# A hand-written timetable taken through the change of token halves, operand blocks replaced in pairs, and the gelu moved behind a copy

## The chip, the core and the metric

The kernel runs on one core of one Trainium2 chip. The metric is device time in microseconds of one execution, the median of three runs; 2668.45 us before the change.

## What is computed

One layer of a hybrid encoder on 2048 tokens of width 1024, in float32. After a mixer (three head groups and an output projection) comes a gated convolutional MLP, and it is there that the change lies:

```python
def conv_ffn(x, w_up, conv_w, conv_b, w_down):
    u = causal_dwconv(x @ w_up, conv_w, conv_b)      # width 3 along the tokens
    g, v = jnp.split(u, 2, axis=-1)                  # 2816 columns each
    return (jax.nn.gelu(g) * v) @ w_down
```

## The kernel before, in words

The up-projection `x @ w_up` is `phase_u` (from L1551). Its work is cut into 44 **units**: two halves of 1024 tokens, 22 column blocks in each (`NFF` = 22), in the order 0, 11, 1, 12, ..., 10, 21. A unit multiplies one block of weights with one half of the tokens, by Winograd's variant of Strassen's scheme: seven products instead of eight, on operands named a11, a12, a22 (blocks of the tokens) and s1, s2, s4, s3 (their sums, stored earlier in DRAM as `summed`), with weights b11, b21, T4, T1, T2, b22, T3 (T1 to T4 are differences). Each operand is held as a high part (`hi`, made by ScalarE, ACT) and a low part (`lo`, the rest, made by VectorE, DVE, or GpSimd, POOL), and each product of 4 x 128 rows is three matmuls per row block (`split3`, L108 to L110), so a unit is 7 x 4 x 3 = 84 matmuls. Results go to PSUM banks X, Y, V and Z. X is used three times and Z twice in a unit: ACT copies a bank out (`keep`, L1775: p1, p5, u2, u3) before the next product may overwrite it. DVE adds the rest (`evac`, L1785). Then come the convolution (ACT L1801, four DVE taps L1741 or L1743), gelu (ACT L1814), the gate product (DVE L1817), and, on every second unit, four sums for the down-projection (L1854 to L1866) and the stores to `aS` (L1632).

The order of all this is written by hand: `steady(first, end)` collects events with a time in ticks (28 ticks are one unit), sorts them by that time, and issues them in that order under `manual_schedule`. The ticks are no clock: they fix only the order of the instructions in each engine's queue, and every engine takes its queue strictly in that order. For unit n, with t0 = 28n and t1 = 28(n + 1), `unit_events` puts the copy p5 at t0 + 16, the copy u2 at t0 + 20, the first bank sum that needs u2 at t0 + 24.2; and, in the next unit's time, gelu at t1 + 13, the gate at t1 + 15.2 and the store of the gated block at t1 + 17. `weight_events` loads and splits the weights of the next unit in the same way; `aux_events` makes, beside chosen units, the operand sums of the second half (units `PRE_U`) and the differences of w_down (22 blocks, one in each of units 20 to 41, `PRE_D_AT`).

This timetable covers units 1 to 20 and 23 to 42. Unit 0 and the last are special. The two around the change of halves, 21 and 22, are `single` units: their seven products run in another order (s1, s2, s4, s3 first; `Product.unit` with `sums_first`), and their instructions are ordered by the general scheduler. While unit 21 runs, `next_half(n)` is called after each product and replaces the operand just used by that of the second half: 28 blocks of 128x512, each loaded, split into hi and lo. The operands have one buffer each, so a block can be replaced only once unit 21 has read it, and must be ready when unit 22 needs it.

Loads go through SyncE's (SP's) queue, and land in shared buffers: four of 512 KB (tag `raw`), six of 256 KB (tag `T`).

Of the kernel before, what the change touches and what calls it, by code (L numbers as in the profile page):

```python
# [18 lines left out]
TH = 1024  # L19
# [3 lines left out]
NFF = DFF // P  # L23
# [39 lines left out]
def tile_hymba_layer(ctx: ExitStack, tc: tile.TileContext, io, out, scr):  # L63
    nc = tc.nc
# [397 lines left out]
    late = []  # L462
# [942 lines left out]
    first = phase_i()  # L1405
# [145 lines left out]
    def phase_u(prod, post_14, post_15):  # L1551
# [12 lines left out]
        def next_half(n):  # L1564

            if n[0] == "s":
                prod.summed_of(1, n)
            else:
                for k in range(4):
                    prod.block(1, k, n, nc.gpsimd if k % 2 else nc.vector)  # L1570

        wT = dram.tile([NFF, P, 4, 512], F32, name="wT", tag="wT")
        w = prod.weights(uw, io["wup_u"][0], "uw0_0", False, ("b21", "b22"), save=wT[0])
        prod.summed_of(0, "s1")
# [131 lines left out]
                for u in range(2):  # L1706
                    products(0, u, (j,))

        def prediffs(ps_, j):

            r, t = (
                rp.tile([P, 4, 256], F32, name=f"p{ps_}_{j}{n}", tag="raw", bufs=prod.raws) for n in "rT"
            )
            nc.sync.dma_start(r, io["wdn"][ps_, j])
            winograd_diffs(t, r[:, 0], r[:, 3], r[:, 1], r[:, 2])
            return lambda: nc.sync.dma_start(scr["diffs"][ps_, j], t)

        order = [b for j in range(NJ) for b in (j, NJ + j)]
        N = NHALF * NFF
        W_ = {0: w}  # L1720
# [2 lines left out]
            half, at = divmod(n, NFF)  # L1723
            return half, at, order[at], f"u{half}_{order[at]}"

        def sums_first(n):
            return n in (NFF - 1, NFF)

        def prepare(n):

            half, _, b, _ = where(n)
            first = sums_first(n)
            W_[n] = prod.weights(
                uw, io["wup_u"][b], f"uw{half}_{b}", first, ("T4",) if first else (),
                wT[b] if half else None, None if half else wT[b],
            )

        def conv_taps(half, u, c, blk, sh):
# [11 lines left out]
        def unit_events(n, at):  # L1750
# [73 lines left out]
            at(t1 + 6.3, tap, 1, 2)  # L1824
            at(t1 + 8.3, tap, 0, 1)
            at(t1 + 10.2, tap, 0, 2)
            at(t1 + 13, gelu)
            at(t1 + 15.2, gate)
            for t, f in operand_steps(half, b, st):
                at(t1 + t, f)  # L1830

        def operand_steps(half, b, st):

            j = b % NJ
            h = slice(0, 4)
# [36 lines left out]

            if b < NJ:
                return [(17, keep)]
            return [(17, store_blocks), (17.2, s3), (18.2, s1), (19.2, s2), (22, s4), (25, store_sums)]

        def weight_events(n, at):

            half, pos, b, _ = where(n)
            nm = f"uw{half}_{b}"  # L1880
            t0 = 28 * (n - 1)
            w = W_[n] = {}
            st = {}

            def load():
                for name, ks in (("ra", slice(0, 2)), ("rb", slice(2, 4))):
                    st[name] = rp.tile([P, 2, 512], F32, name=nm + name, tag="raw", bufs=prod.raws)
                    nc.sync.dma_start(st[name], io["wup_u"][b, :, ks])
                st.update(b11=st["ra"][:, 0], b21=st["ra"][:, 1], b22=st["rb"][:, 0], b12=st["rb"][:, 1])

            def load_t():
                for i in (3, 0, 1, 2):
                    t = rp.tile([P, 512], F32, name=f"{nm}T{i + 1}", tag="T", bufs=prod.raws + 2)
                    nc.sync.dma_start(t, wT[b, :, i])
                    st[f"T{i + 1}"] = t
# [18 lines left out]
            early = 5 if sums_first(n) else 0  # L1914
            if half:
                at(t0 - 28 + 21, load_t)
            else:
                at(t0 + 1.7 - early, diff, "T1", "b12", "b11")
                at(t0 + 2.4 - early, diff, "T2", "b22", "T1")
                at(t0 + 3.1 - early, diff, "T4", "T2", "b21")  # L1920
                at(t0 + 12.2 - 2 * early, diff, "T3", "b22", "b12")
                at(t0 + 5.1, store_t, 1, 2, 4)
                at(t0 + 13.1, store_t, 3)
            names = ("T1", "T2", "b22", "T3", "b11", "T4", "b21") if early else (
                "b11", "b21", "T4", "T1", "T2", "b22", "T3"
            )
            for i, (name, th, tl) in enumerate(zip(
                names, (-1, 2.5, 5, 7, 11, 15, 19), (0, 4.0, 6.2, 8.2, 12.1, 16.5, 20.2)
            )):
                at(t0 + th, hi, name)  # L1930
                at(t0 + tl, lo, name, nc.vector if i else nc.gpsimd)

        def aux(n):


            half, at = divmod(n, NFF)
            if half == 0 and at in PRE_U:
                return "sums", PRE_U.index(at)
            if 0 <= n - PRE_D_AT < len(PRE_D):
                return "diffs", PRE_D[n - PRE_D_AT]  # L1940
            return None

        def aux_events(n, at):
# [48 lines left out]
            at(t0 + 26, make)  # L1992
            at(t0 + 28 + 3, store)

        def steady(first, end):

            ev = []
# [7 lines left out]
                    aux_events(n, at)  # L2005
            for n in range(first + 1, end + 1):
                weight_events(n, at)
            with tc.manual_schedule():
                for _, _, f, args in sorted(ev, key=lambda e: e[:2]):
                    f(*args)  # L2010

        def single(n, after):

            half, at, b, nm = where(n)
            store = None
            if aux(n):
                store = prediffs(*aux(n)[1]) if aux(n)[0] == "diffs" else None
            if n + 1 not in W_:
                prepare(n + 1)
            res = []  # L2020
            for c_, blk in zip(prod.unit(prod.hp, W_[n], nm, after, sums_first(n)), (b, NFF + b)):
# [9 lines left out]
            sums_ = operand(half, b, ug)  # L2031
            for st in (store, sums_):
                if st is not None:
                    st()
# [343 lines left out]
```

## Time and profile before

| what | value |
|---|---|
| median of three runs (lowest, highest) | 2668.45 us (2665.23, 2673.2) |
| the profiled execution's own time | 2669.64 us |
| its span, first to last instruction | 2667.9 us |
| mean granted TensorE clock (1 = full) | 0.974 |
| busy: PE, DVE, ACT, POOL | 93%, 76%, 52%, 30% of the span |
| units 2 to 20, 21 to 23, 24 to 43 of the up-projection | 379.54, 87.97, 403.13 us |

An engine's busy time is the union of its instructions; "idle before" is the time an engine stood still ahead of an instruction, with what released it. Where two neighbouring instructions of one engine overlap in the trace, the start-to-start distance is what the queue pays. A name such as `u_9p` is the tile p of column block 9: digits behind the name are left out, so p1 and p5 both read `u_9p`, and u2 and u3 `u_9u`.

### The profile page before, as it was taken

The numbers are of one execution on the slowest core, as the hardware profiler recorded it, in microseconds if no ns is written. First come the engines' busy times: TensorE is split into PE (matmuls) and PEld (weight loads), VectorE is DVE, ScalarE is ACT, GpSimd is POOL, SyncE is SP. The second block draws the span as 40 slices with busy tenths as digits, with TensorE's granted clock in tenths as the row PEclk, the third lists the DMA queues.
The fourth block names the chain that finished last, engine by engine and source line by source line (L and its number), as shares of the span: only waits on it lengthen the run. The fifth ranks groups of instructions, "written<-read, shape, count | busy, mean of one in ns | idle before, by whom it ended". The sixth has DMA issues, their size and how long they took to land.

```text
span 2667.9 us, 38630 instructions
## 1 busy us (share of the span) xinstructions
PE 2469.9 (93%) x13658; PEld 2122.9 (80%) x13658; DVE 2015.5 (76%) x3086; ACT 1396.6 (52%) x2472; POOL 792.4 (30%) x636
## 2 busy tenths in 40 slices
PE   8899989899888899999899999889999998999997
PEld 8677877778788878878687777677777778999997
DVE  6898689857889864465888888878787877557676
ACT  5556555544567775555544544544444445445343
POOL 5554444434344431132300000521111143003222
PEclk9899989999999999999999999899999999999999
DMA  7444643246666564575545555665666558768776
GB/s 248 147 153 138 206 153 114 93 143 197 169 170 188 169 202 156 172 254 186 192 140 193 183 164 186 225 213 193 207 198 206 194 189 309 236 205 270 272 261 204
DMA packets 316115, 513.55 MB, mean 192 GB/s; under 512 B 23649, under 2 KB 199009, under 8 KB 315921
## 3 DMA queue, kind: packets, MB, share of 16 engines
q1 hardware_dynamic: 314928, 507.94, 58.9%
q8 instruction: 107, 1.75, 0.3%
q0 software_dynamic: 704, 2.10, 0.2%
q10 hardware_dynamic: 288, 1.05, 0.1%
q14 instruction: 88, 0.71, 0.1%
HBM read 343.49 MB, written 167.51 MB: 192 GB/s over the span
## 4 chain that ended last, share of the span: by engine, by line
PE 24%; DVE 13%; DMA 8%; issue 5%; ACT 4%; POOL 1%; SPq 0%; DVEq 0%; ACTq 0%; POOLq 0%
DMA e_10a<-aS 1%; PE e_4b L110 1%; PE mix L109 1%; PE mix L110 1%; PE mix L108 1%; PE e_4b L108 1%; PE e_7b L108 1%; PE e_4b L109 1%; PE e_7b L109 1%; PE e_7b L110 1%; DVE e_6l L2100 1%; PE e_3b L110 1%; PE e_3b L108 0%; PE e_3b L109 0%; PE e_2b L110 0%
## 5 line engine op out<-in xcount | busy, mean ns | idle before, releaser
L996 POOL TENSOR_TENSOR yn<-yn,yg 128x512 f32<-128x512 f32 x16 | 21.6, 1352 | 145.1 <-DMA yg<-gate 103.5
L2190 POOL TENSOR_TENSOR o<-o,y 128x512 f32<-128x512 f32 x14 | 24.6, 1758 | 126.6 <-DVE y L2189 25.4
L108 PE MATMUL mix<-wo,ym 128*128 128x512 f32 x128 | 51.8, 405 | 1.6 <-DVE ysl L1027 1.6
L110 PE MATMUL mix<-wo,ym 128*128 128x512 f32 x128 | 51.0, 398 | 0.0
L109 PE MATMUL mix<-wo,ym 128*128 128x512 f32 x128 | 50.6, 395 | 0.0
L109 PE MATMUL mix<-wol,ysh 128*128 128x512 f32 x128 | 50.4, 394 | 0.1
L110 PE MATMUL mix<-woh,ysl 128*128 128x512 f32 x128 | 50.0, 390 | 0.0
L108 PE MATMUL mix<-woh,ysh 128*128 128x512 f32 x128 | 49.7, 393 | 0.1
L2084 POOL TENSOR_TENSOR d_0l<-d_0r,d_0h 128x768 fp32r<-128x768 f32 x2 | 4.2, 2104 | 145.6 <-DVE e_6y L2166 144.2
L1509 DVE TENSOR_TENSOR bh<-hT,g 128x512 f32<-128x512 f32 x32 | 20.7, 686 | 34.0 <-PE hT L1508 34.0
L1027 DVE TENSOR_TENSOR ym<-yT,ym 128x512 fp32r<-128x512 f32 x16 | 11.0, 689 | 35.6 <-ACT ym L1026 35.6
L2100 DVE TENSOR_TENSOR e_10l<-e_10a,e_10h 128x896 fp32r<-128x896 f32 x15 | 16.4, 1091 | 25.5 <-ACT e_10h L2099 25.5
L998 DVE TENSOR_TENSOR yn<-yn,yg 128x1024 f32<-128x1024 f32 x16 | 21.3, 1332 | 18.5 <-ACT yg L997 18.5
L2099 ACT ACTIVATE e_8h<-e_8a 128x896 fp32r<-128x896 f32 x15 | 14.3, 954 | 38.6 <-DMA e_8a<-aS 30.1
L851 ACT ACTIVATE no<-n 128x256 f32<-128x256 f32 x64 | 23.9, 375 | 16.2 <-PE n L110 7.0
L1498 ACT ACTIVATE bt<-bx 128x1024 f32<-128x1024 f32 x16 | 16.9, 1058 | 29.4 <-DVE bx L1497 29.4
L627 PE MATMUL xT<-ident,x 128*128 128x128 f32 x128 | 20.4, 306 | 12.5 <-DVE x L621 8.4
L628 DVE TENSOR_TENSOR hT<-xT,par 128x512 f32<-128x512 f32 x32 | 21.4, 683 | 13.6 <-PE xT L627 13.6
L2100 DVE TENSOR_TENSOR e_6l<-e_6a,e_6h 128x896 fp32r<-128x896 f32 x15 | 23.8, 1589 | 8.3 <-ACT e_6h L2099 8.3
L1270 DVE SCALAR_TENSOR_TENSOR s_1L<-s_1A,gt,nmask 128x128 f32<-128x128 f32 x64 | 29.2, 482 | 1.0 <-PE s_1pp L1330 0.9
L2100 DVE TENSOR_TENSOR e_9l<-e_9a,e_9h 128x896 fp32r<-128x896 f32 x15 | 16.4, 1091 | 17.5 <-ACT e_9h L2099 17.5
L2100 DVE TENSOR_TENSOR e_5l<-e_5a,e_5h 128x896 fp32r<-128x896 f32 x15 | 23.9, 1596 | 7.4 <-ACT e_5h L2099 7.3
(9832 smaller groups left out, 10909.4 us busy)
## 6 DMA issues: line engine op xcount, KB each, us to landing
x<-in_x_dram SPq DMA_DIRECT2D x16, 512.0 KB, 4.9
hT<-hT SPq DMA_DIRECT2D x16, 512.0 KB, 4.2
gate<-no SPq DMA_DIRECT2D x64, 128.0 KB, 3.0
yn<-yns SPq DMA_DIRECT2D x16, 512.0 KB, 4.6
yg<-gate SPq DMA_DIRECT2D x16, 512.0 KB, 4.9
bx<-in_x_dram SPq DMA_DIRECT2D x16, 512.0 KB, 4.3
x<-bx SPq DMA_DIRECT2D x16, 512.0 KB, 2.9
h2T<-bh SPq DMA_DIRECT2D x16, 512.0 KB, 4.9
```

The costliest lines, as they stand in the source:

```text
L108: a = nc.tensor.matmul(pss, lh, rh, start=first, stop=False, skip_group_check=True)
L109: nc.tensor.matmul(pss, lh, rl, start=False, stop=False, skip_group_check=True)
L110: nc.tensor.matmul(pss, ll, rh, start=False, stop=last, skip_group_check=True)
L627: nc.tensor.transpose(pt[:, j * P : (j + 1) * P], xt[:, k * P : (k + 1) * P], ident)
L628: nc.vector.tensor_tensor(hT[:, 4 * q : 4 * q + 4], pt.rearrange("p (a b) -> p a b", a=4), col(par, "g1", 4 * q, 4).unsqueeze(2).to_broadc ...
L851: nc.scalar.activation(o, pt[:, 0:256], AF.Copy)
L996: nc.gpsimd.tensor_tensor(yn[:, 512:], yn[:, 512:], g[:, 512:], op=ALU.mult)
L998: nc.vector.tensor_tensor(yn, yn, g, op=ALU.mult)
L1270: nc.vector.scalar_tensor_tensor(L[j][:, hd, :], A[:, hd, j, :], ga[:, hd, 2 * g0 + j : 2 * g0 + j + 1], nmask, op0=ALU.subtract, op1=ALU.add,
L1509: nc.vector.tensor_tensor(hT[:, q * 4 : q * 4 + 4, :], pt.rearrange("p (a b) -> p a b", a=4), g2[:, 4 * q : 4 * q + 4].unsqueeze(2).to_bro ...
L2100: nc.vector.tensor_tensor(al, a, ah.bitcast(F32), op=ALU.subtract)
L2190: nc.gpsimd.tensor_tensor(o[i][:, hs], o[i][:, hs], t, op=ALU.add)
```

## The change

Five things:

1. `steady(1, N - 1)` now covers units 1 to 42 without a break. The two `single` units around the change of halves and their other order of products go.
2. A new `next_half(at)` puts the replacement of the 28 operand blocks into the timetable, as 14 pairs, 3.5 ticks apart, from tick 2.2 of unit 21. A pair's load is issued 7 ticks before its first hi; of every three pairs two use a `raw` buffer, one two `T` buffers; 23 lo parts go to DVE and 5 to POOL.
3. Gelu moves from t1 + 13 to t1 + 16.4, behind p5 and ahead of u2; the gate from 15.2 to 18; the store of the gated block from 17 to 19.5; the sums close up between 19.6 and 22.
4. In the second half the loads of the weight differences are issued one by one (T4, T1, T2, T3 at t0 - 5, - 3, + 1, + 8) instead of together, and the second weight load leaves out b12, which is not used there. For units 22 to 24 the weight loads come later.
5. The differences of w_down are made beside units 16, 18, 19 and 23 to 41 instead of 20 to 41.

The diff, cut to its core:

```diff
-PRE_D, PRE_D_AT = [(i, j) for i in range(2) for j in range(11)], 20
+PRE_D = [(i, j) for i in range(2) for j in range(11)]
+PRE_D_AT = (16, 18, 19) + tuple(range(23, 42))
...
-            at(t1 + 13, gelu)
-            at(t1 + 15.2, gate)
+            at(t1 + 16.4, gelu)
+            at(t1 + 18, gate)
...
-            return [(17, store_blocks), (17.2, s3), (18.2, s1), (19.2, s2), (22, s4), (25, store_sums)]
+            return [(19.5, store_blocks), (19.6, s3), (20.2, s1), (20.8, s2), (22, s4), (25, store_sums)]
...
-            at(t0 - 28 + (9 if aux(n - 3) else 2), load)
+            late = NFF <= n <= NFF + 2
+            t_load = t0 - 28 + (9 if aux(n - 3) else 2)
+            at(t0 - 9 if late else t_load, load, "ra", slice(0, 2), ("b11", "b21"))
+            at(
+                t0 - 2 if late else t_load + 0.1, load, "rb", slice(2, 3 if half else 4),
+                ("b22",) if half else ("b22", "b12"),
+            )
             if half:
-                at(t0 - 28 + 21, load_t)
+                for i, t in ((4, -5), (1, -3), (2, 1), (3, 8)):
+                    at(t0 + t, load_t, i)
...
+        def next_half(at):
+            for i in range(14):
+                name, ks = ("a11", "a12", "a22", "s1", "s2", "s4", "s3")[i // 2], (2 * (i % 2), 2 * (i % 2) + 1)
+                t = 28 * (NFF - 1) + 2.2 + 3.5 * i
...
+                at(t - 7, load)
+                at(t, hi, 0)
+                at(t + 0.9, hi, 1)
+                at(t + 0.9, lo, 0, nc.vector)
+                at(t + 1.8, lo, 1, nc.gpsimd if i % 3 == 1 else nc.vector)
...
         single(0, finish_b)
-        steady(1, NFF - 1)
-        single(NFF - 1, next_half)
-        single(NFF, None)
-        steady(NFF + 1, N - 1)
+        steady(1, N - 1)
```

## Rows read from the trace of the kernel before

**Rows 1.** Page: span of the profiled execution

```profile
span 2667.9 us, 38630 instructions
```

**Rows 2.** Windows: stretch, length, PE, PEld, DVE, ACT, POOL busy, PEclk, DMA, GB/s

```profile
1307.93:1687.47 379.54, 370.77 (x1598) 301.33 (x1597) 325.57 (x418) 178.34 (x303) 26.61 (x19) 0.99 0.52 170
1687.47:1775.44 87.97, 70.53 (x254) 52.64 (x252) 71.06 (x74) 42.47 (x71) 50.69 (x33) 0.83 0.75 247
1775.44:2178.57 403.13, 391.71 (x1683) 314.20 (x1682) 324.09 (x393) 188.67 (x324) 57.32 (x47) 1.00 0.61 198
```

**Rows 3.** Windows of single units of the up-projection

```profile
1404.46:1423.77 19.31, 19.31 (x86) 15.78 (x85) 14.76 (x19) 9.43 (x16) 1.29 (x1) 1.00 0.62 203
1443.07:1468.37 25.30, 22.30 (x85) 17.66 (x84) 17.43 (x23) 9.31 (x16) 1.27 (x1) 0.87 0.71 233
1566.52:1589.01 22.49, 19.61 (x86) 15.69 (x85) 17.44 (x23) 9.31 (x16) 1.29 (x1) 1.00 0.80 258
1627.62:1648.85 21.23, 19.64 (x85) 15.70 (x84) 20.38 (x27) 9.32 (x16) 1.68 (x1) 1.00 0.60 199
1706.75:1752.12 45.37, 28.69 (x85) 19.07 (x83) 42.94 (x44) 22.66 (x36) 26.91 (x16) 0.74 0.74 246
1752.12:1775.44 23.32, 22.56 (x85) 17.79 (x85) 12.19 (x14) 9.51 (x19) 14.08 (x10) 0.84 0.65 220
1814.14:1834.30 20.16, 19.62 (x86) 15.69 (x84) 17.58 (x24) 9.32 (x16) 2.42 (x3) 1.00 0.56 181
1834.30:1854.30 20.00, 19.61 (x86) 15.69 (x84) 15.04 (x19) 9.32 (x16) 2.39 (x3) 1.00 0.72 236
```

**Rows 4.** Waits of PE outside the switch: total, times, longest

```profile
PE u_15Z L108 <- ACT u_15p L1775: 3.0, 1, 3.0
...
PE u_17Z L108 <- ACT u_17p L1775: 1.5, 1, 1.5
```

**Rows 5.** Waits of PE, 1690 to 1775 us

```profile
PE u_11X L108 <- ACT uw_11b11h L131: 6.6, 1, 6.6
PE u_0W L109 <- DVE uS_3s4l L133: 5.4, 1, 5.4
```

**Rows 6.** Timeline of unit 18: start us, length, engine, line

```profile
1639.76 1.27 DVE L1743 SCALAR_TENSOR_TENSOR u_19v<-u_19ca,upar,u_19v 128x1022 f32<-128x1022 f32 x1
1641.12 1.06 ACT L1814 ACTIVATE u_19v<-u_19v 128x1024 f32<-128x1024 f32 x1 [4.76 <-DVE u_19v L1743]
1642.09 0.61 ACT L1908 ACTIVATE uw_20b22h<-uw_20rb 128x512 fp32r<-128x512 f32 x1
1642.61 0.58 ACT L1775 ACTIVATE u_9p<-u_9Z 128x512 f32<-128x512 f32 x1
1643.24 0.50 PE L108 MATMUL u_9Z<-uS_0s4h,uw_9b22h 128*128 128x512 f32 x1 [1.59 <-ACT u_9p L1775]
1643.61 0.59 ACT L1775 ACTIVATE u_9u<-u_9X 128x512 f32<-128x512 f32 x1
```

**Rows 7.** Timeline of DVE in unit 30

```profile
1894.22 0.42 DVE L99 TENSOR_TENSOR x29t<-x29r 128x256 f32<-128x256 f32 x1 [1.02 <-DMA x29r<-in_wdn_dram]
1895.71 1.40 DVE L102 TENSOR_TENSOR x29t<-x29t,x29r 128x256 f32<-128x256 f32 x1
...
1908.28 1.23 DVE L1817 TENSOR_TENSOR u_14v<-u_14v,u_14v 128x1024 f32<-128x1024 f32 x1 [0.52 <-ACT u_14v L1814]
...
1912.88 0.69 DVE L1866 TENSOR_TENSOR u_14v<-u_14v,u_3v 128x512 f32<-128x512 f32 x1
```

**Rows 8.** Line L133, 1690 to 1776 us: min/median/max ns

```profile
L133 POOL TENSOR_TENSOR uw_0T2l<-uw_0T,uw_0T2h x1: 1472/1472/1472, 1697.9 to 1697.9; 128x512 fp32r<-128x512 f32 x1
...
L133 DVE TENSOR_TENSOR uA_0a11l<-uA_0a,uA_0a11h x1: 679/679/679, 1711.3 to 1711.3; 128x512 fp32r<-128x512 f32 x1
...
L133 DVE TENSOR_TENSOR uA_2a11l<-uA_2a,uA_2a11h x1: 1768/1768/1768, 1716.2 to 1716.2; 128x512 fp32r<-128x512 f32 x1
```

**Rows 9.** DMA issues, 1776 to 2179 us: KB, us to landing

```profile
aS<-us SPq DMA_DIRECT2D x10, 256.0 KB, 6.9
```

More of the change, by code (lines that the diff above doesn't have):

```diff
@@ L1563, in phase_u @@
         prod.sp, prod.rp, prod.kp = us.get, rp, up
[L1564 to L1570, printed above, removed]
         wT = dram.tile([NFF, P, 4, 512], F32, name="wT", tag="wT")
@@ L1724, in where @@
             return half, at, order[at], f"u{half}_{order[at]}"
-        def sums_first(n):
-            return n in (NFF - 1, NFF)
         def prepare(n):
             half, _, b, _ = where(n)
-            first = sums_first(n)
             W_[n] = prod.weights(
-                uw, io["wup_u"][b], f"uw{half}_{b}", first, ("T4",) if first else (),
-                wT[b] if half else None, None if half else wT[b],
+                uw, io["wup_u"][b], f"uw{half}_{b}", diffs=wT[b] if half else None, save=None if half else wT[b]
             )
@@ L1873, in operand_steps @@
             if b < NJ:
-                return [(17, keep)]
-            return [(17, store_blocks), (17.2, s3), (18.2, s1), (19.2, s2), (22, s4), (25, store_sums)]
+                return [(19.5, keep)]
+            return [(19.5, store_blocks), (19.6, s3), (20.2, s1), (20.8, s2), (22, s4), (25, store_sums)]
         def weight_events(n, at):
@@ L1883, in weight_events, with load, load_t @@
             st = {}
[L1885 to L1895, printed above, removed]
+            def load(name, ks, names):
+                t = rp.tile([P, 2, 512], F32, name=nm + name, tag="raw", bufs=prod.raws)
+                nc.sync.dma_start(t[:, 0 : ks.stop - ks.start], io["wup_u"][b, :, ks])
+                st.update((n, t[:, i]) for i, n in enumerate(names))
+            def load_t(i):
+                t = rp.tile([P, 512], F32, name=f"{nm}T{i}", tag="T", bufs=prod.raws + 2)
+                nc.sync.dma_start(t, wT[b, :, i - 1])
+                st[f"T{i}"] = t
             def diff(name, x, y):
@@ L1911, in lo @@
                 eng.tensor_tensor(w[name][1], st[name], w[name][0].bitcast(F32), op=ALU.subtract)
-            at(t0 - 28 + (9 if aux(n - 3) else 2), load)
-            early = 5 if sums_first(n) else 0
+            late = NFF <= n <= NFF + 2
[5 more added lines that the diff above has]
+            )
             if half:
-                at(t0 - 28 + 21, load_t)
-            else:
[L1918 to L1921, printed above, removed]
+                for i, t in ((4, -5), (1, -3), (2, 1), (3, 8)):
+                    at(t0 + t, load_t, i)
+            else:
+                at(t0 + 1.7, diff, "T1", "b12", "b11")
+                at(t0 + 2.4, diff, "T2", "b22", "T1")
+                at(t0 + 3.1, diff, "T4", "T2", "b21")
+                at(t0 + 12.2, diff, "T3", "b22", "b12")
                 at(t0 + 5.1, store_t, 1, 2, 4)
                 at(t0 + 13.1, store_t, 3)
-            names = ("T1", "T2", "b22", "T3", "b11", "T4", "b21") if early else (
-                "b11", "b21", "T4", "T1", "T2", "b22", "T3"
-            )
             for i, (name, th, tl) in enumerate(zip(
-                names, (-1, 2.5, 5, 7, 11, 15, 19), (0, 4.0, 6.2, 8.2, 12.1, 16.5, 20.2)
+                ("b11", "b21", "T4", "T1", "T2", "b22", "T3"),
+                (-1, 2.5, 5, 7, 11, 15, 19), (0, 4.0, 6.2, 8.2, 12.1, 16.5, 20.2)
             )):
@@ L1938, in aux @@
                 return "sums", PRE_U.index(at)
-            if 0 <= n - PRE_D_AT < len(PRE_D):
-                return "diffs", PRE_D[n - PRE_D_AT]
+            if n in PRE_D_AT:
+                return "diffs", PRE_D[PRE_D_AT.index(n)]
             return None
@@ L1993, in aux_events, with load, hi, lo @@
             at(t0 + 28 + 3, store)
+        def next_half(at):
+            for i in range(14):
+                name, ks = ("a11", "a12", "a22", "s1", "s2", "s4", "s3")[i // 2], (2 * (i % 2), 2 * (i % 2) + 1)
+                nm = f"uB{name}{ks[0]}"
+                st = {}
+                t = 28 * (NFF - 1) + 2.2 + 3.5 * i
+                def load(name=name, ks=ks, nm=nm, st=st, split=i % 3 == 2):
+                    if split:
+                        st["r"] = [
+                            rp.tile([P, 512], F32, name=f"{nm}r{q}", tag="T", bufs=prod.raws + 2) for q in range(2)
+                        ]
+                    else:
+                        r = rp.tile([P, 2, 512], F32, name=nm + "r", tag="raw", bufs=prod.raws)
+                        st["r"] = [r[:, q] for q in range(2)]
+                    if name[0] == "s":
+                        src = prod.summed[1, int(name[1]) - 1, :, ks[0] : ks[1] + 1]
+                    else:
+                        y, x = int(name[1]) - 1, int(name[2]) - 1
+                        src = prod.src[
+                            4 * x + ks[0] : 4 * x + ks[1] + 1, :, TH + 512 * y : TH + 512 * y + 512
+                        ].rearrange("k p t -> p k t")
+                    if split:
+                        for q in range(2):
+                            nc.sync.dma_start(st["r"][q], src[:, q])
+                    else:
+                        nc.sync.dma_start(r, src)
+                def hi(q, name=name, ks=ks, nm=nm, st=st):
+                    pool = prod.sp(name) if name[0] == "s" else prod.hp
+                    prod.H[ks[q]][name] = [
+                        pool.tile([P, 512], F32R, name=f"{nm}{q}{x}", tag="H" + name, bufs=8) for x in "hl"
+                    ]
+                    nc.scalar.activation(prod.H[ks[q]][name][0], st["r"][q], AF.Copy)
+                def lo(q, eng, name=name, ks=ks, st=st):
+                    h, l = prod.H[ks[q]][name]
+                    eng.tensor_tensor(l, st["r"][q], h.bitcast(F32), op=ALU.subtract)
+                at(t - 7, load)
[3 more added lines that the diff above has]
+                at(t + 1.8, lo, 1, nc.gpsimd if i % 3 == 1 else nc.vector)
         def steady(first, end):
@@ L2007, in steady @@
                 weight_events(n, at)
+            next_half(at)
             with tc.manual_schedule():
@@ L2014, in single @@
             half, at, b, nm = where(n)
[L2015 to L2019, printed above, removed]
+            prepare(n + 1)
             res = []
-            for c_, blk in zip(prod.unit(prod.hp, W_[n], nm, after, sums_first(n)), (b, NFF + b)):
+            for c_, blk in zip(prod.unit(prod.hp, W_[n], nm, after), (b, NFF + b)):
                 res.append(
@@ L2030, in single @@
             nc.vector.tensor_tensor(ug, ug, uv, op=ALU.mult)
[L2031 to L2034, printed above, removed]
+            operand(half, b, ug)
         single(0, finish_b)
-        steady(1, NFF - 1)
-        single(NFF - 1, next_half)
-        single(NFF, None)
-        steady(NFF + 1, N - 1)
+        steady(1, N - 1)
         last(W_[N - 1], where(N - 1)[3], 1, where(N - 1)[2])
```

7 lines of the change are left out of this document (removed).

## The prediction

> **What bounds the kernel now.** I read the page for the span [rows 1], then the busy time by stretch [rows 2], then single units [rows 3], then what PE waited for [rows 4, 5], and last the timelines behind the two kinds of wait [rows 6, 7].
>
> In the up-projection PE sets the pace. An undisturbed unit takes 19.31 us with PE busy all of it [rows 3], so a tick is worth 19.31 / 28 = 0.69 us. What a stretch takes beyond that is loss [rows 2]: units 2 to 20 lose 379.54 - 19 x 19.31 = 12.7 us; units 21 to 23, around the change of halves, 87.97 - 3 x 19.31 = 30.0 us; units 24 to 43 lose 403.13 - 20 x 19.31 = 16.9 us. Together 59.6 us, and only there can the change gain.
>
> The 12.7 and 16.9 us have one cause: PE waits at bank Z for p5, up to 3.0 us in the first half and 1.5 us in the second [rows 4]. Unit 18 shows why [rows 6]. It starts at 1627.62. Z is complete at tick 16, at 1638.7, and PE needs it empty at tick 20, at 1641.4. But ACT has gelu ahead of p5; gelu stands behind the last tap on DVE and starts at 1641.12, 13.5 us into the unit. Then come gelu, one hi and p5, which ends at 1643.19, and PE has stood for 1.59 us.
>
> The 30.0 us are another thing [rows 5]: PE waits for the new operands' low parts (5.4 us for one of them) and 6.6 us for the weights of unit 23. In unit 22 PE is busy 28.69 of 45.37 us at a granted clock of 0.74, and in unit 23 the clock is 0.84 [rows 3].
>
> **Gelu behind p5.** No work is added; ACT's queue is reordered. p5 can now run at tick 16, 2.8 us before it is due: this wait goes. Next in line is u2. It waits for tick 20 and is due at tick 24, 16.55 us into the unit, and ahead of it now stand gelu (0.97 us start to start), a hi (0.52 us) and its own 0.59 us [rows 6]. So gelu may start as late as 16.55 - 2.08 = 14.5 us. Unit 18's 13.5 us passes. Unit 9 waited 1.4 us more than unit 18 (3.0 against 1.6), so its gelu came at about 14.9 and u2 would be 0.4 us late; unit 15, with 22.49 - 19.61 = 2.9 us idle [rows 3], likewise. In the second half no wait is above 1.5 us, so every gelu there passes. The gate moves back with gelu; two low parts of DVE now run before it instead of waiting behind it, so DVE loses nothing.
>
> The store of the gated block now leaves two sums closer to s4, which overwrites its source. Now s4 begins 3.4 us after the gate's end without a wait [rows 7]; one instruction of 0.69 us fewer lies between, so DVE may stand 0.7 us on every second unit. DVE is busy 17.58 us in such a unit of 20.16 [rows 3], so that is hidden.
>
> **Differences beside units 16, 18, 19.** Each costs DVE 1895.71 + 1.40 - 1894.22 = 2.9 us [rows 7]. Unit 18's stretch already has DVE busy 20.38 of 21.23 us. Bounds: nothing (units 16 and 20 absorb it) to 2.9 us once; I take 1, nearer to nothing because units whose predecessor keeps only a block have 19.31 - 14.76 = 4.6 us of DVE free [rows 3].
>
> **Loads of the differences T and of b22.** T4, T1, T2 keep 10 ticks, 6.9 us, between load and hi, T3 11 ticks; a 256 KB transfer to DRAM lands in 6.9 us there [rows 9]. I cost them at 0 to 3 us over the half and take 2; the cover is that spacing, and without it T1's low part and all taps behind it on DVE slip. b12 left out saves 256 KB a unit and no time.
>
> So the first half gains 12.7 - 0.8 - 1 = 10.9 us and the second 16.9 - 2 = 14.9 us.
>
> **The change of halves.** The seven products run in their usual order, and a pair is due 2 ticks after the one before it but made 3.5 ticks after it: pair 0 has some 25 ticks in hand, pair 13 about 5, or 3.7 us. The question is DVE. One unit's regular work on it, with the 2.8 us of w_down differences (which units 20 to 22 no longer make) taken out, is 15.04 - 2.8 = 12.2 us, or 17.58 - 2.8 = 14.8 us with the four sums [rows 3, 7]; units 21 and 22 together 27.0 us. The 28 blocks add 23 low parts at 0.68 us [rows 8] = 15.6 us. The five on POOL are not free: a low part on DVE beside one on POOL took 1.77 us, not 0.68 [rows 8], so each may hold DVE up 1.1 us, 5.5 us in all. The sum is 27.0 + 15.6 + 5.5 = 48.1 us of work for 2 x 19.31 = 38.6 us. Nearly all of it stands ahead of pair 13's low parts, so PE stops about 9.5 us in all, in the later products of unit 22 (first through gelu and u2, whose taps are late, then through the operands). ACT is no bound: 2 x 9.32 us [rows 3] and 28 hi parts of 0.52 us make 33.2 of 38.6 us. Stops cost clock: unit 9 stood 3.0 us and lost 6.0 at a clock of 0.87, unit 15 stood 2.9 and lost 3.2 at 1.00 [rows 3]; I add 3 us. SP's loads stand behind the gated block's store and wait for buffers that DVE frees, 0.5 us more. The 6.6 us for weights go: these now have a whole unit of lead. Residue 13 us of 30.0, a gain of 17.
>
> Bounds of the residue: below, 27.0 + 28 x 0.61 (start to start of such parts without POOL in the way) - 38.6 = 5 us, less 3 if the waits that DVE now has between conv and taps are filled: 2 us. Above, every second low part blocked as in [rows 8]: 27.0 + 28 x 1.2 - 38.6 = 22 us, and 5 for the clock: 27 us.
>
> The Trainium skill, "SBUF — State Buffer", section "Who interferes with whom", speaks against the five parts on POOL: a DVE operation with two SBUF inputs and a GpSimd one exclude each other for the whole instruction, the later waits. By that, five POOL instructions of 1.47 us [rows 8] would hold DVE for 7.4 us, not 5.5, and the time would be 2 us higher.
>
> **Sum.** 10.9 + 14.9 + 17.0 = 42.8 us off. The profiled execution took 2669.64 us (span 2667.9 [rows 1] and 1.7 us around it), 1.2 us above the median shown. 2669.64 - 42.8 - 1.2 gives 2625.6; I say 2626 us. With the residues' bounds, (12.7 - 4) + (16.9 - 5) + 3 = 24 to 12.7 + 16.9 + 28 = 57.6 us off, it would be 2611 to 2645.
>
> **Rivals.**
> - *The replacement hides wholly.* DVE fills its present gaps (it idles 87.97 - 71.06 = 17 us in the three units even now [rows 2]) and POOL holds nothing up. Against: 27.0 + 15.6 alone is 4 us over. Gain 10.9 + 14.9 + 28: 2615 us.
> - *The switch gains almost nothing.* A pair's buffer is freed only by its low part, the next load waits for the buffer, and a late DVE delays loads, hi parts on ACT and so its own next work. For it: 44 instructions kept DVE busy 42.94 us in unit 22 [rows 3]. Against: that included sums on another order. It decides once a pair takes over 12 ticks from load to low part. Gain 25.8 + 3: 2640 us.
> - *Gelu moves the stall instead of removing it.* If the taps slip by over 1 us in most units, u2 takes p5's place and the two halves gain nothing: 17 us off, 2651 us. For it: DVE's new neighbours. Against: 13.5 us where 14.5 is allowed.
> - *Slower: s4 stands behind the store.* Place: DVE's s4, every second unit, now closer behind the gated block's store. In unit 30 that store had landed within 3.4 us of the gate's end [rows 7], but other stores to the same tensor took 6.9 us [rows 9]. At 6.9, s4 waits 4 us, gelu comes some 3 us later and u2 is up to 2 us late: 20 such units lose 40 us, just what the halves and switch gain. It turns the sign when the store needs over about 8 us: 43 us are to be eaten, 2.2 us in each. At 9 us: 60 us lost, 2685 us.
> - *The change does not do what it says* (the queues keep their old order): none of the times moves, 2668 us. The sort by ticks speaks against it.
>
> **How the numbers follow.** Forecast 0.52; hidden wholly 0.18; switch gains nothing 0.14; stall moved 0.06; slower 0.06; no effect 0.04. A measurement of this kernel can tell about 0.3%, 8 us, from no change. All cases but the last two are faster by more: 0.90; same 0.04; slower 0.06. The range 2609 to 2645 holds the first three cases with their bounds, some 0.82.
>
> **What would show it.** Right: no wait of PE for p5 or u2 above 0.5 us; units 2 to 20 and 24 to 43 within 2 us of 39 x 19.31; unit 21 at 19 to 20.5 us, unit 22 at 29 to 33 us with PE waiting for low parts of s2, s4 and s3, or for u2; unit 23 near 19.3. Wrong: PE waits for u2 in most units; DVE idle on a DMA before s4; unit 22 under 23 us, or over 40.

## The result, and the profile after

The changed kernel takes 2642.22 us (median of four runs, 2638.97 to 2645.18) against 2670.1 us of the kernel before beside it (2665.23 to 2673.2): a ratio of 0.9881, 95% interval 0.9859 to 0.9904, so about 28 us faster. The forecast was 2626 us, the range 2609 to 2645: the sign and the range held, the size was 16 us too good.

All of it lies in the up-projection. The windows of the three stretches, and below them of single units, after the change (columns as in [rows 2]):

```profile
1312.47:1687.89 375.42, 369.60 (x1598) 300.55 (x1597) 325.77 (x424) 180.69 (x303) 28.03 (x21) 1.00 0.56 179
1687.89:1764.18 76.29, 65.55 (x254) 50.95 (x252) 60.31 (x77) 43.84 (x79) 20.49 (x10) 0.91 0.71 233
1764.18:2150.51 386.33, 386.33 (x1683) 315.64 (x1682) 309.90 (x394) 193.45 (x324) 52.96 (x47) 1.00 0.62 195
...
1447.62:1468.99 21.37, 19.60 (x86) 15.70 (x85) 18.48 (x25) 9.42 (x16) 1.74 (x1) 1.00 0.70 228
1565.52:1589.06 23.54, 21.20 (x86) 16.87 (x85) 18.48 (x25) 9.42 (x16) 1.68 (x1) 0.93 0.74 229
1687.89:1713.75 25.86, 22.22 (x85) 17.60 (x84) 21.59 (x29) 16.89 (x30) 8.77 (x3) 0.87 0.88 284
1713.75:1744.49 30.74, 23.64 (x85) 17.29 (x84) 25.16 (x31) 17.30 (x33) 9.69 (x6) 0.90 0.62 210
1744.49:1764.18 19.69, 19.69 (x86) 16.06 (x84) 13.56 (x18) 9.65 (x16) 2.03 (x2) 0.98 0.63 202
```

Less 19.31 us a unit (19.307 unrounded, which moves a stretch's loss by 0.1 us at most), the stretches now lose 8.5 us (units 2 to 20), 18.4 (21 to 23) and 0.2 (24 to 43, where PE is busy in every microsecond); before it was 12.7, 30.0 and 16.9 [rows 2]. That is 32.6 us off. Units 21 to 23, with the change of halves in them, are called the switch from here on. The span shrank by 30.8 us: the part ahead of unit 2, in which no instruction changed, came out 4.5 us longer in this execution, the rest 2.7 us shorter. The start of unit 2 lay between 1307.9 and 1326.1 us in the executions of this study, so below the kernels are compared by these three losses, and the total stands beside them. The changed kernel and two of the experiments (e4, e7) have the same instructions in units 2 to 20; they lost 8.5, 7.6 and 8.1 us there, so a difference under 1 us between two single executions says nothing.

What is left shows in PE's waits after the change, first outside the switch, then in it (total, times, longest; compare [rows 4, 5]):

```profile
PE u_18X L109 <- ACT u_18u L1754: 2.3, 1, 2.3
PE u_15X L109 <- ACT u_15u L1754: 1.8, 1, 1.8
PE u_20X L109 <- ACT u_20u L1754: 1.6, 1, 1.6
...
PE u_21Z L109 <- ACT u_21p L1754: 3.6, 1, 3.6
PE u_0X L110 <- DVE uBs320l L2015: 3.6, 1, 3.6
PE u_0Z L110 <- DVE uBs400l L2015: 2.0, 1, 2.0
```

No wait for p5 (bank Z) is left outside the switch. In its place stand three for u2 (bank X), in units 9, 15 and 19. In the switch, unit 21 waits for p5, and unit 22 for low parts of s4 and s3.

The timeline around unit 9 shows where u2's lateness begins. Queue of SP, then DVE, ACT and PE, after the change (start us, length, engine, line):

```profile
1441.32 0.37 SPq L1955 DMA_DIRECT2D x8r<-h2T  x1
1441.79 0.40 SPq L1955 DMA_DIRECT2D x8t<-h2T  x1
1442.64 0.37 SPq L1625 DMA_DIRECT2D aS<-u_14v  x1
...
1449.16 0.69 DVE L1845 TENSOR_TENSOR u_14v<-u_14v,u_3v 128x512 f32<-128x512 f32 x1 [2.93 <-DMA aS<-u_14v]
...
1463.82 1.06 ACT L1793 ACTIVATE u_4v<-u_4v 128x1024 f32<-128x1024 f32 x1 [3.76 <-DVE u_4v L1722]
...
1466.13 0.50 PE L109 MATMUL u_15X<-uS_0s3h,uw_15T3h 128*128 128x512 f32 x1 [1.77 <-ACT u_15u L1754]
```

And SP's queue at the same place before the change:

```profile
1437.56 0.37 SPq L1632 DMA_DIRECT2D aS<-u_14v  x1
1438.03 0.45 SPq L1974 DMA_DIRECT2D x8r<-h2T  x1
1438.57 0.89 SPq L1974 DMA_DIRECT2D x8t<-h2T  x1
```

The store of the gated block (`aS<-u_14v`) used to be issued ahead of the 1 MB of loads of the side work (x8r, x8t). Moved from tick 17 to 19.5, it stands behind them, which are at 17.5. The sum s4 (L1845) overwrites the store's source: issued at 1442.64, the store let it start at 1449.16, 6.5 us later, and DVE stood for 2.93 us. The taps slip, gelu starts 1463.82 - 1447.62 = 16.2 us into unit 9, and u2 behind it is late. This reading, that a swap of two DMAs in one queue did as much as the moved gelu, is what the first experiments test.

### The profile page after: what moved, and what is told of

Read it like the earlier page. It is cut to its first block, busy times and chain, and to the rows that moved or that the text cites. A ratio compares the mean times of both kernels' runs of the same rounds, so it can differ in the third digit from the quotient of the medians.

```text
span 2637.1 us, 38638 instructions
## 1 busy us (share of the span) xinstructions
PE 2459.5 (93%) x13658; PEld 2122.8 (80%) x13658; DVE 1986.0 (75%) x3096; ACT 1404.5 (53%) x2480; POOL 759.5 (29%) x616
## 5 line engine op out<-in xcount | busy, mean ns | idle before, releaser
L2119 DVE TENSOR_TENSOR e_10l<-e_10a,e_10h 128x896 fp32r<-128x896 f32 x15 | 16.4, 1090 | 23.3 <-ACT e_10h L2118 23.2
L1499 ACT ACTIVATE bt<-bx 128x1024 f32<-128x1024 f32 x16 | 16.9, 1059 | 29.4 <-DVE bx L1498 29.4
L852 ACT ACTIVATE no<-n 128x256 f32<-128x256 f32 x64 | 23.8, 374 | 16.2 <-PE n L111 5.9
L998 ACT ACT_TABLE_LOAD x16 | 20.5, 1283 | 19.7 <-DMA yg<-gate 19.5
L2119 DVE TENSOR_TENSOR e_9l<-e_9a,e_9h 128x896 fp32r<-128x896 f32 x15 | 16.4, 1090 | 17.6 <-ACT e_9h L2118 17.6
```

The costliest lines, as they stand in the source:

```text
L852: nc.scalar.activation(o, pt[:, 0:256], AF.Copy)
L998: nc.scalar.activation(g, g, AF.Sigmoid)
L2119: nc.vector.tensor_tensor(al, a, ah.bitcast(F32), op=ALU.subtract)
```

## The experiments

All losses in us, as above; "beside" is the time of the kernel before, run beside it. One run each, but five for the last. Each experiment is named by the first part of its label, as e1.

| kernel | time | beside | units 2-20 | 21-23 | 24-43 |
|---|---|---|---|---|---|
| before, profiled | 2669.64 | | 12.7 | 30.0 | 16.9 |
| changed, profiled | 2638.97 | | 8.5 | 18.4 | 0.2 |
| e1_gelu_only | 2651.48 | 2679.0 | 6.7 | 31.2 | 0.2 |
| e2_switch_only | 2673.03 | 2679.0 | 19.0 | 16.6 | 21.0 |
| e3_load_behind | 2670.14 | 2679.0 | 10.3 | 18.3 | 18.2 |
| e4_no_low | 2631.24 | 2679.0 | 7.6 | 7.4 | 1.6 |
| e8_order_only | 2653.44 | 2671.29 | 20.4 | 15.4 | 0.3 |
| e5_s4_late | 2637.88 | 2671.29 | 0.0 | 16.8 | 0.2 |
| e6_gelu_u2 | 2629.78 | 2671.29 | 2.7 | 12.6 | 0.2 |
| e7_all_dve | 2633.53 | 2671.29 | 8.1 | 15.4 | 0.2 |
| e9_s4_dve | 2635.01 | 2678.1 | 0.0 | 14.7 | 0.2 |
| e10_defer | 2621.24 | 2678.1 | 0.0 | 9.3 | 0.2 |
| e11_loads_first | 2622.13 | 2678.68 | 0.0 | 7.6 | 0.2 |

**Part 3 alone, in the kernel before (e1).**

```diff
-            at(t1 + 13, gelu)
-            at(t1 + 15.2, gate)
+            at(t1 + 16.4, gelu)
+            at(t1 + 18, gate)
-                return [(17, keep)]
-            return [(17, store_blocks), (17.2, s3), (18.2, s1), (19.2, s2), (22, s4), (25, store_sums)]
+                return [(19.5, keep)]
+            return [(19.5, store_blocks), (19.6, s3), (20.2, s1), (20.8, s2), (22, s4), (25, store_sums)]
```

> Only part 3 of the change (gelu behind p5, gate, store and sums later), on the kernel before. Theory (the first half's residue comes from s4, which waits for the store of the gated block, because the loads of the side work now stand ahead of that store in SP's queue): units 2 to 20 lose 5 to 8 us, at units 9 and 15, and nothing worth naming at 12 and 18; units 24 to 43 lose 0 to 3; units 21 to 23 lose 28 to 32 as before. Rival (the residue comes from the w_down differences moved beside units 16, 18 and 19, which this kernel doesn't move): units 2 to 20 lose under 2 us.

The second half's loss is gone (0.2), the first half keeps 6.7, with waits for u2 in units 9 and 15 (2.3 and 2.4 us), the switch is as before (31.2). So part 3 makes all of the second half's gain and the first half's residue too; the other parts add 8.5 - 6.7 = 1.8 us in units 2 to 20.

**All but part 3 (e2)**: the changed kernel with gelu, gate, stores and sums at their old ticks (the diff of part 3 turned round).

> The change without part 3: gelu, gate, store and sums where they were before. Theory (the two parts add up): units 24 to 43 lose 14 to 18 us again and units 2 to 20 lose 12 to 17; units 21 to 23 lose 18 to 25, since p5 behind gelu costs there too. Rival (the second half's gain comes from the loads of T and of b22 issued one by one, not from gelu): units 24 to 43 lose under 6.

The switch loses 16.6 us without the moved gelu: its gain is the new replacement's own. Both halves came out worse than expected, and worse than before (19.0 and 21.0): with gelu ahead of p5 the other parts cost some 6 and 4 us. That these are the differences of w_down beside units 16, 18 and 19 in the first half, and the separate loads of T in the second, is argued; no run parts them.

**The side work's loads put behind the store again (e3)**, gelu left where the change has it:

```diff
-            at(t0 + 17.5, load)
+            at(t0 + 19.9, load)
```

> The change, with the loads of the side work (sums of the second half, differences) at tick 19.9 instead of 17.5, so behind the store of the gated block. Theory (s4 waits for that store because those loads are ahead of it): DVE's wait before s4 falls from 2.9 us to under 1, units 2 to 20 lose under 4 us instead of 8.5; units 21 to 23 stay at 16 to 20. Rival (DVE is simply overfull beside units 8, 14, 16, 18, 19): they lose 7 to 10 as in the change.

Half right. s4's wait is gone in units 8 and 14 (2.9 and 3.5 us in the changed kernel) and falls from 3.3 and 2.1 to 1.4 and 0.7 us in units 16 and 18, so the loads ahead of the store did make it. But the loss of units 2 to 20 rose to 10.3 us. Units 9 and 15 lose 1.5 and 1.6 us instead of 2.1 and 4.2, but units 18 and 20 lose 4.0 and 2.4, where DVE now waits 3.6 and 4.4 us for the side work's loads, and the whole second half is lost again (18.2). There DVE waits for the side work's load in every unit, 0.8 to 4.0 us, and s4 for the store in every second, 0.7 to 2.7 us. DVE's timeline in that kernel, at the longest of these waits:

```profile
1892.75 0.43 DVE L100 TENSOR_TENSOR x29t<-x29r 128x256 f32<-128x256 f32 x1 [3.96 <-DMA x29r<-in_wdn_dram]
```

3.96 us, where the kernel before waited 1.02 [rows 7]. So the order of these two DMAs has a price on either side: the loads behind the store make DVE wait for the loads, ahead of it, in the first half, they make s4 wait for the store.

**The new order with the old gelu (e8)**: the changed kernel with only

```diff
-            at(t1 + 16.4, gelu)
-            at(t1 + 18, gate)
+            at(t1 + 13, gelu)
+            at(t1 + 15.2, gate)
```

> The change with gelu and gate back at 13 and 15.2, but the stores and sums left late (19.5 and on), so that the side work's loads still stand ahead of the gated block's store in SP's queue. Theory from the load moved behind the store, which cost the second half 18.2 us (the second half's gain comes from these loads being ahead of the store, whatever gelu's place): units 24 to 43 lose under 5 us, and the gelus there start some 11.5 us into their units. Rival (it comes from gelu behind p5, as predicted): they lose 10 to 20 us, waiting for p5. Both: units 2 to 20 lose 10 to 18, at p5.

The window of units 24 to 43 of this kernel:

```profile
1776.35:2162.76 386.41, 386.41 (x1683) 315.51 (x1682) 311.69 (x394) 191.89 (x325) 60.53 (x47) 1.00 0.62 195
```

With gelu ahead of p5, as before, the second half loses 0.3 us; gelu starts 11.1 to 11.7 us into units 24 to 42, where before it started 11.7 to 13.4 us into units 25 to 42. The first half loses 20.4, more than the 10 to 18 expected. The four kernels e2, e8, e3 and the changed one make a square (first half / second half):

| | store ahead of the loads | loads ahead of the store |
|---|---|---|
| gelu ahead of p5 | 19.0 / 21.0 | 20.4 / 0.3 |
| gelu behind p5 | 10.3 / 18.2 | 8.5 / 0.2 |

In the first half gelu's place is worth 9 to 12 us and the order 1 or 2 either way; in the second half the order is worth 18 to 21 us and gelu's place at most 3. The lower left corner is not clean: with gelu the gate stands 2.8 ticks later there, and the store and the load behind it go out later with it, so what gelu's place alone would be worth in the second half is not shown. That the order alone suffices there is: 21.0 to 0.3. SP's queue in the second half shows why, after the change:

```profile
1884.19 0.33 SPq L1938 DMA_DIRECT2D x30r<-in_wdn_dram  x1
1894.26 0.38 SPq L1625 DMA_DIRECT2D aS<-u_14v  x1
```

and before it:

```profile
1909.53 0.38 SPq L1632 DMA_DIRECT2D aS<-u_14v  x1
1910.01 0.45 SPq L1957 DMA_DIRECT2D x30r<-in_wdn_dram  x1
```

The store waits for the gate, and the load behind it with it. Ahead of the store the load goes out 10 us before it, and DVE no longer waits for it.

**s4 later (e5)**, so that the store lands before it:

```diff
-            return [(19.5, store_blocks), (19.6, s3), (20.2, s1), (20.8, s2), (22, s4), (25, store_sums)]
+            return [(19.5, store_blocks), (19.6, s3), (20.2, s1), (20.8, s2), (27, s4), (29.5, store_sums)]
```

> The change with s4 at tick 27 instead of 22, behind the side work's sums, and the stores of the sums at 29.5 instead of 25. Theory (the first half's residue is DVE standing at s4 for the gated block's store): units 2 to 20 lose under 2.5 us instead of 8.5; units 24 to 43 lose under 1; units 21 to 23 lose 12 to 17 instead of 18.4, since the pairs' loads no longer stand behind the stores of the sums. Rival (DVE has too much to do beside units 8, 14, 16 to 20): units 2 to 20 still lose 6 to 9.

The window of units 2 to 20 of this kernel:

```profile
1319.53:1686.36 366.83, 366.83 (x1597) 299.65 (x1596) 327.92 (x426) 182.10 (x304) 29.08 (x22) 1.00 0.57 184
```

19 units of 19.31 us: nothing is lost, and PE never stops. The residue of the first half was s4's wait, all of it. Unit 21 falls from 25.86 to 21.58 us as well, since in unit 20 s4 and the stores of the sums no longer stand ahead of the switch's work; units 22 and 23 take 32.32 and 20.85, so of that only 1.6 us stays.

**Gelu behind u2 (e6)** (20.4, gate 22, stores 23.4, sums 23.5 to 25, s4 30), the rival cure.

> The change with gelu one copy further back, behind u2 (tick 20.4), the gate at 22, the stores from 23.4, s4 at 30 and the sums' stores at 32. Theory (all that is left outside the change of halves is u2 behind a late gelu): units 2 to 20 and 24 to 43 lose under 2 us together; units 21 to 23 lose 10 to 15, as their copies wait for no tap any more but the low parts and late loads stay. Rival (the next copy, u3, takes over the wait): they lose 6 us or more at a matmul that waits for u3 or for a bank.

First half 2.7 us (units 9, 15 and 19 wait 0.6 us for u2 each), a little over the 2 us expected; switch 12.6. For the two halves s4's place is the better cure. That the switch gains because DVE's regular work of unit 21 now stands behind more of the new operands' low parts is argued, since s4 and the stores moved too.

**The switch: low parts left out (e4).** The 28 `lo` instructions go, and their tiles are those of the high parts.

> The change, with the low parts of the 28 replaced operand blocks left out (the high part stands in for them in the products, so the second half is computed with wrong low parts; all matmuls stay). Theory (units 21 and 22 are bound by VectorE's work): units 21 to 23 lose 3 to 9 us instead of 18.4. Rival (they are bound by when the pairs' loads arrive, behind other work in SP's queue): they lose 12 to 18.

Units 21 and 22 of this kernel:

```profile
1692.49:1717.35 24.86, 21.09 (x86) 16.81 (x84) 14.01 (x17) 16.93 (x30) 1.30 (x1) 0.93 0.97 304
1717.35:1738.53 21.18, 19.89 (x86) 15.63 (x84) 13.80 (x18) 17.19 (x33) 2.98 (x2) 1.00 0.81 274
```

Unit 22 loses 1.9 us instead of 11.4: it is bound by the low parts, by DVE's time for them or by the buffers that they hold (without them a buffer comes free at its hi); this run does not part the two. Unit 21 still takes 24.86 us and still waits 3.8 us for p5: that is something else.

**All 28 low parts on DVE (e7).**

```diff
-                at(t + 1.8, lo, 1, nc.gpsimd if i % 3 == 1 else nc.vector)
+                at(t + 1.8, lo, 1, nc.vector)
```

> The change with all 28 low parts of the replaced operands on DVE, none on POOL. Theory (a low part on POOL holds DVE up about as long as it would take DVE itself): units 21 to 23 lose 15 to 20 us, within 3 of the 18.4. Rival (the five parts on POOL are work taken off DVE, 5 x 0.68 us): they lose 21 us or more. A third way (POOL's parts, up to 6.3 us long, hold buffers and loads): they lose under 15.

The switch loses 15.4 us instead of 18.4, at the low end of the theory's range and close to the third way's. POOL's five parts help nothing, and cost some 3 us.

**s4 late and all low parts on DVE (e9).**

> The change with both mends that paid alone: s4 at 27 with the sums' stores at 29.5 (units 2 to 20 lost nothing, units 21 to 23 16.8 us), and all 28 low parts on DVE (units 21 to 23 15.4 us). If they add up: units 2 to 20 lose under 1, units 24 to 43 under 1, units 21 to 23 12 to 15 us. If DVE's work alone sets the end there (theory), units 21 to 23 stay at 13 to 16, because the first mend only moves the wait from unit 21 to unit 22.

0.0 / 14.7 / 0.2 us. The 14.7 lies in both ranges and decides nothing, but the single units speak for the theory: against e7, unit 21 loses 4.5 us less (2.3 against 6.8), and units 22 and 23 lose 3.8 us more. On top of the low parts on DVE the late s4 gains 0.7 us in the switch; on top of the late s4 (16.8) the low parts gain 2.1.

**DVE work moved out of the way (e10)**: on top of that, gelu, gate, stores and sums in unit 22's time 10 ticks later, and four low parts of unit 23's weights 8 ticks later.

```diff
+            d = 10 if n == NFF - 1 else 0
-            at(t1 + 16.4, gelu)
-            at(t1 + 18, gate)
+            at(t1 + 16.4 + d, gelu)
+            at(t1 + 18 + d, gate)
             for t, f in operand_steps(half, b, st):
-                at(t1 + t, f)
+                at(t1 + t + d, f)
...
-                at(t0 + tl, lo, name, nc.vector if i else nc.gpsimd)
+                at(t0 + tl + (8 if n == NFF + 1 and i > 2 else 0), lo, name, nc.vector if i else nc.gpsimd)
```

> As the run before, and unit 21's gelu, gate, stores and sums 10 ticks later, and four low parts of unit 23's weights 8 ticks later, so that some 5.8 us of DVE's work (gate 1.2, sums 2.8, three low parts 1.8) stand behind the last pair instead of ahead of it, and u2 of unit 22 waits for no gelu. Nothing is left out. Theory (units 21 and 22 are bound by DVE's work ahead of the last pair): units 21 to 23 lose 5 to 6 us less than the run before, 6 to 10 us. Rival (by when the pairs' loads land and their buffers come free): within 2 us of the run before.

The switch loses 9.3 us, 5.4 less, for 5.8 us of DVE work moved behind the last pair. Nothing leaves the kernel; it only runs where unit 23 has DVE free.

**Loads before a store that waits (e11).** In unit 21 SP issues the keep store of block 10 ahead of the load of s1's second pair, and that store waits for the gate; the load of unit 23's weights ahead of both waits for a buffer. On top of e10:

```diff
-                return [(19.5, keep)]
+                return [(24 if half == 0 and b == order[NFF - 2] else 19.5, keep)]
...
-            at(t0 - 9 if late else t_load, load, "ra", slice(0, 2), ("b11", "b21"))
+            at((t0 - 6.5 if n == NFF + 1 else t0 - 9) if late else t_load, load, "ra", slice(0, 2), ("b11", "b21"))
```

> As the run before, and in SP's queue the store of unit 20's gated block (now at 24) and the first weight load of unit 23 (now 6.5 ticks ahead instead of 9) stand behind the load of the eighth pair, so that this load waits for its buffer alone and not for the gate on DVE. Theory (what is left in units 21 to 23 is this late load, for which ACT stood 5.1 us): ACT's wait falls to 1 to 3 us and units 21 to 23 lose 5 to 8 us instead of 9.3. Rival (DVE's work still sets the end): 8 to 10 us as before. The whole: units 2 to 43 lose under 9 us of the 59.6 before, so the kernel takes 46 to 54 us less than the one before the change, and 16 to 25 us less than the change.

ACT's wait for that pair, in this kernel's timeline:

```profile
1715.74 0.64 ACT L2012 ACTIVATE uBs120h<-uBs12r 128x512 fp32r<-128x512 f32 x1 [1.52 <-DMA uBs12r<-summed]
```

and in e10:

```profile
1708.63 0.63 ACT L2012 ACTIVATE uBs120h<-uBs12r 128x512 fp32r<-128x512 f32 x1 [5.06 <-DMA uBs12r<-summed]
```

The switch loses 7.6 us instead of 9.3: unit 22 falls from 26.26 to 22.78 us, unit 21 rises from 21.64 to 23.43. Timed in five runs against nine of the kernel before: 2622.13 us (2614.22 to 2628.15) against 2678.68, a ratio of 0.9786, interval 0.976 to 0.9811. That is 56.6 us less, where 46 to 54 were expected, though the three stretches lose 7.8 us as expected (under 9). It beats both kernels (the change itself stands at 0.9881, and the intervals lie apart); whether it beats e10, at 2621.24 in one run, can't be told from these runs.

## Why the prediction was right or wrong

| step | forecast gain | measured |
|---|---|---|
| units 2 to 20 | 10.9 | 12.7 - 8.5 = 4.2 |
| units 24 to 43 | 14.9 | 16.9 - 0.2 = 16.7 |
| units 21 to 23 | 17.0 | 30.0 - 18.4 = 11.6 |
| sum | 42.8 | 32.5 |

The measured time lies in the range, but at its upper end: 16 us above the forecast and 2 us from the time of the rival "The switch gains almost nothing" (2640 us), which is not what happened, since the switch gained 11.6 us. Of the three stretches two gained less than forecast (6.7 and 5.4 us less) and one 1.8 us more; the rest of the 16 us lies outside them.

*Gelu's limit was right.* It said that gelu may start 14.5 us into a unit. In units 9, 15 and 19 it started at 16.2, 16.8 and 16.0, that is 1.7, 2.3 and 1.5 us past it, and PE waited 1.8, 2.3 and 1.6 us. What failed is the claim that no gelu would be much later than that.

*First half: the failed step is the store costed at nothing* ("DVE may stand 0.7 us on every second unit ... that is hidden"). The step counted the DVE instructions between gate and s4 and looked at a unit of the second half [rows 7]. It did not go through SP's queue past which the store is moved: from 17 to 19.5, past 17.5, where the side work's loads stand. Their 512 KB or 1 MB went out 0.9 to 1.3 us ahead of the store in units 8, 14, 16 and 18, and DVE stood 2.9, 3.5, 3.3 and 2.1 us there (2.0 in unit 20, behind a load of weights); units 9, 15 and 19 lost 8.2 us by it. e5 leaves 0.7 and 1.3 us of such waits in two units, and the loss is 0. The rival "s4 stands behind the store" had named the place and the mechanism. It was priced for all the units of a kind, from the landing time of another store [rows 9]; it occurs in five units of the first half, and once, for 1.0 us and at no cost, in the second, where the load goes out 10 us ahead of the store and is out of its way.

*The differences beside 16, 18 and 19* were put at 1 us of DVE's work; the change loses 1.8 us more than e1, which does not make them there. The size agrees by luck: e5, which does make them there, loses nothing in units 2 to 20, so DVE had room for the work, and the 1.8 us (unit 19) are s4's wait behind their loads.

*Second half: right in size by luck, wrong in cause.* The step laid the 16.9 us to gelu ahead of p5. The square shows that there the swap of load and store does it (21.0 to 0.3 with the old gelu), and that gelu behind p5 does little while the load stays behind the store (21.0 to 18.2). PE's wait at bank Z [rows 4] was real, and gelu did stand ahead of p5; but gelu was late there because DVE had waited for the w_down load (in e8, without that wait, p5 costs nothing), in the row that the prediction itself used to price the differences [rows 7: 1.02 us]. It read that row's length and passed over its wait. The 2 us for the loads of T were not needed: 0.2 is left, which is the last unit's own 19.50 us.

*The switch, by the forecast's terms.* They were 9.5 us of stops by DVE, 0.5 by SP's loads, and 3 for the clock. After the change PE stands 76.29 - 65.55 = 10.7 us in units 21 to 23. That this sum fits is luck: unit 21, forecast at 19 to 20.5 us, stops 3.6 us, and unit 22 7.1 of its 9.5. The term of the sum that was most off is the clock: PE is busy 65.55 us with the matmuls of three units, 7.6 us more than 3 x 19.31, at granted clocks of 0.87, 0.90 and 0.98 in the three units. These are means of two levels: in the windows 1704.5 to 1711.0, 1731.8 to 1735.0 and 1742.0 to 1745.2 the clock is 0.50 (1.2 of 2.4 GHz), and 1.00 in those between them. Each of the three begins within about 1 us of the end of a stop of PE (3.64, 1.99 and 3.58 us). The 3 us were taken from units with one stop each [rows 3].

*The switch, DVE's budget: the work was right.* Regular work of units 21 and 22 was put at 27.0 us; e4, without low parts, has 14.01 + 13.80 = 27.8. With them 48.1 was forecast, and DVE is busy 21.59 + 25.16 = 46.8. Unit 22 took 30.74 us of the 29 to 33 named, with PE waiting for low parts of s4 and s3, as named. 9.5 us of stops and 3 for the clock were 12.5; it lost 11.4, but of these 7.1 are stops and 4.3 slower matmuls (PE busy 23.64 us, granted clock 0.90). And the budget took DVE to be busy all the time: it stood idle 56.60 - 46.75 = 9.85 us in the two units.

*The switch, loads: a term put far too low.* "SP's loads ... 0.5 us more" and unit 21 at 19 to 20.5 us: it took 25.86, a loss of 6.6, of which PE stood 3.6 us for p5. Two stores are in the way. The first is that of s4's sum in unit 20, as the timeline of the changed kernel shows (SP, then ACT):

```profile
1690.49 0.36 SPq L1625 DMA_DIRECT2D aS<-u_20v  x1
...
1692.63 0.42 SPq L2004 DMA_DIRECT2D uBa112r<-h2T  x1
...
1691.70 1.25 ACT L1780 ACTIVATE u_10v<-u_10cb,upar 128x1024 f32<-128x1024 f32 x1 [2.67 <-DVE u_10cb L1764]
...
1698.86 0.63 ACT L2011 ACTIVATE uBa1120h<-uBa112r 128x512 fp32r<-128x512 f32 x1 [2.02 <-DMA uBa112r<-h2T]
...
1704.92 0.58 ACT L1754 ACTIVATE u_21p<-u_21Z 128x512 f32<-128x512 f32 x1
```

s4 had waited 1.96 us and ended late, so the store of its sum was issued at 1690.49, and the loads of weights and pairs stood behind it: the second pair's load went out 4.7 us after the unit's start, and ACT waits 2.02 us for it, after 2.67 us for a bank sum that stands behind s4 on DVE. In e5, where s4 and the stores of the sums stand behind those loads, it went out 1.3 us ahead of the start, and ACT doesn't wait for that pair:

```profile
1685.06 0.43 SPq L2004 DMA_DIRECT2D uBa112r<-h2T  x1
...
1687.98 1.25 ACT L1780 ACTIVATE u_10v<-u_10cb,upar 128x1024 f32<-128x1024 f32 x1 [0.82 <-DVE u_10cb L1764]
...
1700.94 0.58 ACT L1754 ACTIVATE u_21p<-u_21Z 128x512 f32<-128x512 f32 x1
```

p5 starts 17.0 us into unit 21 in the one and 14.6 in the other; the unit loses 6.6 and 2.3 us. e5 moves the sum and its store together (s4 still waits 1.3 us there), so what each does alone is not shown. Nor did the cure bring 4.3 us to the switch: units 22 and 23 gave 2.7 of it back. In e5 ACT still waits 2.9 us in three places for uBa120r and uBa122r, loads issued in a bunch.

The second comes later, the store of unit 20's gated block. The forecast named such a store and priced it, with the buffers, at those 0.5 us:

```profile
1707.95 0.33 SPq L1866 DMA_DIRECT2D uw_11ra<-in_wup_u_dram  x1
1710.30 0.37 SPq L1625 DMA_DIRECT2D aS<-u_10v  x1
1710.71 0.51 SPq L2004 DMA_DIRECT2D uBs12r<-summed  x1
...
1715.85 0.63 ACT L2011 ACTIVATE uBs120h<-uBs12r 128x512 fp32r<-128x512 f32 x1 [5.29 <-DMA uBs12r<-summed]
```

The keep store waits for the gate, which ended at 1710.26, and the pair's load behind it lands 5.1 us after its issue. ACT stands for 5.29 us, and DVE gets its work that much later. e11 takes it away and unit 22 gains 3.5 us over e10, half of which unit 21 gives back.

*POOL's parts.* They were put at 5.5 us of DVE's time, 2.1 us more than the same parts would take on DVE (5 x 0.68). Beside the five parts four DVE instructions are longer than their kind, by 0.69, 0.50, 1.01 and 0.96 us, 3.2 us in all. But e7 gives DVE five more parts, 3.4 us, and the switch is 3 us shorter (2.1 us with s4 late, e9 against e5): the forecast's size held, but not its reason. What DVE lost was not the price; what stands for it is POOL's own duration, which puts the parts late:

```profile
1707.56 6.27 POOL L2015 TENSOR_TENSOR uBa2201l<-uBa220r,uBa2201h 128x512 fp32r<-128x512 f32 x1 [6.18 <-ACT uBa2201h L2011]
...
1726.67 2.69 POOL L2015 TENSOR_TENSOR uBs401l<-uBs40r,uBs401h 128x512 fp32r<-128x512 f32 x1 [7.03 <-ACT uBs401h L2011]
```

That this lateness makes the 3 us is argued, not shown. The rule of the Trainium skill that was weighed there ("SBUF — State Buffer", section "Who interferes with whom": the later of the two waits for the whole instruction) would, with DVE always the later, have had DVE lose 7.4 us. The rows have it lose 3.2, and have one instruction on POOL take 5 us longer than its kind while DVE went on.

## What to carry to other kernels

A DMA that is moved in a hand-written order is moved past every other DMA of its queue: list what stands between its old tick and its new one, and ask of each which engine waits for it; here one swap gave some 20 us in one half, and left 8 us of a new wait in the other that one later sum takes away. In SP's rows a store that waited for its source held back the load behind it (ACT stood 5.29 us), so loads with a deadline go ahead of it, and the instruction that overwrites the store's source goes late. When a wait ends at one engine (p5 on ACT), follow it back once more before pricing its cure: the first lateness may be a short DMA wait in another engine's row. And price stops apart from the slower matmuls that come with them: in the switch the second was 7.6 us beside 10.7 of the first.

## What was not expected of the hardware

- A low part on POOL took 6.27 us where others took 1.29: from 1707.85 to 1713.20 DVE started nine instructions one behind the other, and eight of them kept their usual lengths (0.68 us, the gate 1.21). What grew was POOL's time.
- Loads issued in a bunch in unit 21 (0.88 of the DMA engines' time, 284 GB/s) landed 7.8 to 8.7 us after their issue; the pairs of s4 in unit 22 landed after 3.6 and 3.8 us.
- Two stops of PE of nearly one length went with different clocks: in e1, unit 9 stopped 2.28 us and lost 2.6 at a granted clock of 1.00, unit 15 stopped 2.41 us and lost 4.2 at a mean of 0.93. Unit 9 before had stopped 3.0 us and lost 6.0 [rows 3]; a fixed price of a stop was not to be had from these runs.
